# First norm summed over a host-transposed x, a column table from the host, and natural x loaded late

## The chip, the core and the metric

The kernel runs on one core of one Trainium2 chip. The core has five engines that work side by side and meet by semaphores: TensorE (PE) multiplies matrices, VectorE (DVE) and ScalarE (ACT) work element by element, GpSimd (POOL) does small odd jobs, and SyncE (SP) issues most of the loads. 16 DMA engines move data from memory to the core's SBUF; PE writes its sums to PSUM, in eight banks. The metric is the device time of one run in microseconds (us), lower being better.

## The reference

One decoder layer on 256 tokens with 1024 channels, all in float32. What matters here is its beginning:

```python
def rmsnorm(x, g):
    y = x * rsqrt(mean(x * x, axis=-1) + EPS)
    return y * g
xn = rmsnorm(h, mix_norm_g)
proj = xn @ w_in        # split into aq ak av mq mk mv mo mi mf ga gm
...                     # attention on aq ak av, an mLSTM on mq mk mv mo mi mf
h = h + merged @ w_out  # merged: both mixers, gated by ga and gm
h = h + hierarchical_moe(rmsnorm(h, ffn_norm_g))   # 32 experts, top 2 per token
```

After the experts come a small gated embedding and a last norm. The experts' weights are by far the most of what is read: some 200 of 242 MB.

## The kernel before, in words

The kernel is one straight program, whose order within each engine a scheduler fixes ahead of time: what stands earlier in the text has the higher priority among what its model thinks ready, and each engine then works through its list in order. Large tiles share a ring of ten slots (`slot`, `NRING`); a load into a ring slot waits until all that reads the slot's earlier tile is done. Loads are queued on SP in the order of the text.

*Products in two halves.* Products are made with a rounded format. So each operand is split: ACT writes the rounded upper half (`whi`, `x_hi`), DVE the rest (`wlo`, `x_lo`), and three products (hi·hi, hi·lo, lo·hi) give the sum. One split of a weight tile of 128x512 feeds twelve products of 256 columns, or six of 512. The staging tiles are three of each (`whi`, `wlo`), with two more (`spare`) from aq on.

*The start (lines 65 to 110).* x comes in its natural layout, tokens on partitions, in two halves into `h`, interleaved with the four pieces of mq's weights. Gains and biases come as rows in six small loads (`rows`), the first gain in a seventh (`g1r`), the gate biases in two more (`ifb`). Three warm products (lines 229 to 231) use `identb`, which ACT casts from `ident`.

*mq (lines 234 to 311).* PE turns `g1r` into columns, and transposes x in four groups of four products (`transpose_x`, line 253) into the "tp" banks of PSUM. For each of eight k, ACT and DVE split the transposed x (times the gain) and the weights, and PE makes twelve products into `pmq`, four tiles in PSUM: three "po" banks and one "at" bank. x is not scaled by the norm's factor; that is done when a product is copied out. The helpers `on_act` and `on_dve` chain these steps on their engines. `square_x` (line 275) lets ACT square the natural x into the scratch tile `y` and sum along the row, at k = 2 and 5. `norm_x` (line 280), at k = 6, makes the factor `r1` per token (scaling on DVE, power on POOL), and PE and DVE spread it as rows, `rT`. `load_columns` (line 244) then turns the other gains and biases into columns.

*Behind mq.* Line 548 copies `pmq` out, times `rT`. `if_gates` (line 385) makes the input and forget gates: POOL spreads their weights into the scratch `y`, 24 products go into `pif` (a "po" bank), and a chain of small steps of four partitions on DVE and ACT follows, with two scans and an exponential and a logarithm. `if_columns` (line 412) transposes the result on PE. Then come mk, aq, `conv` 0 to 2, ak, `conv` 3 to 5, av, and attention with the other projections between its heads, the mLSTM, the gates, `w_up`, `w_out` (which reads `h`) and the router. `pif`, mk and all later projections go through `proj_T` (line 323) or `proj_N`, so their splits have line 220 (ACT) and 221 (DVE).

*The experts.* For each of 32 experts 6 MB are loaded into ring slots (`load_expert`, lines 713 and 718), and PE works on them as they come.

## Time and profile before

| | before |
|---|---|
| median of 3 runs | 702.91 us (702.17 to 702.95) |
| the profiled run | 702.59 us |
| its span, first to last instruction | 701.0 us |
| PE, DVE, ACT busy, share of the span | 80%, 40%, 27% |
| moved by DMA | 242.01 MB, mean 345 GB/s |
| the chain that ended last, by engine | DMA 55%, PE 37%, DVE 4% |

All times below are of the profiled run and count from the start of its span. A busy PE is not a PE at its peak, since products are pipelined and their ends are modelled. A share of busy time is a mean over stages with different limits; each stage is read by itself.

### The profile page before, as it was taken

What the parts mean: (1) busy time and instruction counts of PE and PEld (TensorE: products, weight loads), DVE (VectorE), ACT (ScalarE), POOL (GpSimd) and SP (SyncE); (2) the same over time, 40 slices, a digit from 0 to 9 for tenths busy, and PEclk for the clock granted to TensorE, in tenths of its full rate; (3) what the DMA queues carried; (4) which work ended last, traced back from release to release, by engine and by line L of the source; (5) the groups of instructions that cost most, each with busy time, mean ns of one, the idle gap of its engine ahead of it and who ended that gap; (6) DMA issues with size and microseconds to landing.
All of it is one profiled execution on the core that took longest, in us unless ns stands there. A gap on an engine that the chain in (4) does not pass through costs nothing.

```text
span 701.0 us, 12218 instructions
## 1 busy us (share of the span) xinstructions
PE 561.0 (80%) x5161; PEld 381.0 (54%) x5161; DVE 280.6 (40%) x684; ACT 185.9 (27%) x423; POOL 38.2 (5%) x59
## 2 busy tenths in 40 slices
PE   7999999999999998595477574877666975855894
PEld 6899778899986554252233231644323442422384
DVE  4898667676665333041122014323201310401175
ACT  6575556455453211000000000010001110000263
POOL 2000000001300000000000000000000000000063
PEclk9999999999999999799789857799958998988998
DMA  7956533338777899999999999999999999999911
GB/s 252 429 226 246 223 131 121 121 121 326 309 334 301 320 429 424 427 428 425 428 426 425 428 428 424 423 426 426 426 428 421 428 427 426 427 426 426 412 70 61
DMA packets 22134, 242.01 MB, mean 345 GB/s; under 512 B 4708, under 2 KB 5304, under 8 KB 7096
## 3 DMA queue, kind: packets, MB, share of 16 engines
q1 hardware_dynamic: 22056, 241.16, 83.1%
q8 instruction: 42, 0.69, 0.4%
q14 instruction: 20, 0.16, 0.1%
q10 hardware_dynamic: 16, 0.00, 0.0%
HBM read 240.10 MB, written 1.05 MB: 344 GB/s over the span
## 4 chain that ended last, share of the span: by engine, by line
DMA 55%; PE 37%; DVE 4%; ACT 2%; issue 1%; POOL 1%; POOLq 0%; SPq 0%; DVEq 0%; ACTq 0%
DMA wt<-in_expert_gu 32%; DMA wt<-in_expert_down 17%; DMA wpp<-in_w_ple_proj 5%; PE po L331 4%; PE po L332 4%; PE po L333 4%; PE pg L811 3%; PE po L348 2%; PE po L347 2%; PE po L349 2%; PE pd L828 2%; PE px L762 1%; PE ps L840 1%; DMA wt<-in_w_mix 1%; PE pyy L471 1%
## 5 line engine op out<-in xcount | busy, mean ns | idle before, releaser
L811 PE MATMUL pg<-wt,xe 128*32 128x256 f32 x2032 | 157.8, 448 | 70.1 <-DMA wt<-in_expert_gu 70.1
L811 PEld LDWEIGHTS pg<-wt,xe 128*32 128x32 f32 x2032 | 74.5, 125 | 138.8 <-issue 58.6
L828 PE MATMUL pd<-wt,hT 128*32 128x256 f32 x1024 | 72.2, 428 | 17.2 <-DMA wt<-in_expert_down 13.1
L834 DVE COPY eo<-pd 32x256 f32<-32x256 f32 x64 | 27.1, 423 | 107.7 <-ACT eo L836 107.6
L836 ACT ACTIVATE eo<-pd 32x256 f32<-32x256 f32 x64 | 24.0, 374 | 142.2 <-PE pd L828 123.7
L828 PEld LDWEIGHTS pd<-wt,hT 128*32 128x32 f32 x1024 | 38.2, 120 | 40.7 <-issue 24.9
L817 DVE TENSOR_TENSOR hid<-sg,pg 128x128 f32<-128x128 f32 x32 | 9.2, 288 | 125.2 <-ACT sg L815 125.2
L221 DVE TENSOR_TENSOR wlo<-wt,whi 128x512 fp32r<-128x512 f32 x76 | 51.6, 686 | 18.0 <-ACT whi L220 17.7
L220 ACT ACTIVATE whi<-wt 128x512 fp32r<-128x512 f32 x77 | 47.2, 627 | 31.4 <-PE po L349 14.3
L815 ACT ACTIVATE sg<-pg 128x128 f32<-128x128 f32 x32 | 8.9, 278 | 173.1 <-PE pg L811 173.1
L762 PE MATMUL px<-og,y 128*128 128x128 f32 x256 | 37.4, 298 | 11.4 <-DVE og L753 8.0
L762 PEld LDWEIGHTS px<-og,y 128*128 128x128 f32 x256 | 33.7, 207 | 23.5 <-issue 12.7
L840 PE MATMUL ps<-eo,dwT 128*128 128x512 f32 x64 | 34.3, 662 | 8.9 <-DVE eo L834 8.8
L333 PE MATMUL po<-XT,wlo 128*128 128x256 f32 x144 | 40.2, 279 | 1.0 <-DVE wlo L221 1.0
L331 PE MATMUL po<-XT,whi 128*128 128x256 f32 x144 | 40.6, 282 | 0.0
L332 PE MATMUL po<-XT,whi 128*128 128x256 f32 x144 | 40.2, 279 | 0.0
L766 DVE TENSOR_TENSOR xe<-px,cols 128x256 f32<-128x256 f32 x32 | 13.6, 425 | 65.5 <-PE pg L811 44.2
L221 POOL TENSOR_TENSOR glo<-wt,ghi 128x1024 fp32r<-128x1024 f32 x4 | 10.6, 2664 | 446.5 <-ACT ghi L220 446.5
L333 PEld LDWEIGHTS po<-XT,wlo 128*128 128x128 f32 x144 | 27.1, 188 | 1.3 <-DVE wlo L221 1.2
L331 PEld LDWEIGHTS po<-XT,whi 128*128 128x128 f32 x144 | 27.1, 188 | 0.2 <-ACT whi L220 0.2
L221 DVE TENSOR_TENSOR spare<-wt,spare 128x512 fp32r<-128x512 f32 x34 | 23.3, 688 | 9.7 <-ACT spare L220 9.7
L332 PEld LDWEIGHTS po<-XT,whi 128*128 128x128 f32 x144 | 27.1, 188 | 0.2 <-issue 0.2
(371 smaller groups left out, 956.2 us busy)
## 6 DMA issues: line engine op xcount, KB each, us to landing
...
wt<-in_w_mix SPq DMA_DIRECT2D x10, 2048.0 KB, 22.2
...
```

What stands on the lines that cost most here:

```text
L220: a = nc.scalar.activation(dst_hi, src, AF.Copy)
L221: b = (lo_on or nc.vector).tensor_tensor(dst_lo, src, dst_hi.bitcast(F32), op=OP.subtract)
L331: mm(out[:, f], whi[:, kk], ahi[:, k], start=(k == 0), stop=False)
L332: mm(out[:, f], whi[:, kk], alo[:, k], start=False, stop=False)
L333: mm(out[:, f], wlo[:, kk], ahi[:, k], start=False, stop=(k == kn - 1))
L347: mm(outs[b], ahi[:, k, bs], whi[:, k - k0], start=(k == 0), stop=False)
L762: ins = mm(px[:, k], y[:, b, kc:kc + P], og[:, b], start=(b == 0), stop=(b == NB - 1))
L811: ins = pe(mm(pg[32 * j:32 * j + 32], xe[:, k, 32 * i:32 * i + 32], gu[k][:, :, j * P:(j + 1) * P], start=(k == 0), stop=(k == KD - 1)))
L828: pe(mm(pd[32 * c:32 * c + 32], hT[:, 32 * j:32 * j + 32], dn[j][:, c * 256:(c + 1) * 256], start=(j == 0), stop=(j == 3)))
L834: nc.vector.tensor_copy(out=dst, in_=pd[32 * c:32 * c + 32])
L836: nc.scalar.activation(dst, pd[32 * c:32 * c + 32], AF.Copy)
L840: mm(ps, dwT[0:n, b], eo[0:n, c * 512:(c + 1) * 512], start=True, stop=True)
```

## The change

x also comes transposed from the host (`xT`, channels on partitions), in three pieces, between five pieces of mq's weights, into the first half of the ring tile `QK`, which later holds attention's q and k. So PE no longer transposes x for mq. All gains and biases come as one table of columns (`cols`, 128 x 85) on ACT's queue, and the seven loads of rows, the two of the gate biases, and the transposes that made columns go. The cast of `identb` moves from ACT to DVE, and four more warm products are made.

The first norm's sum: ACT squares the transposed x in four pieces (before k = 5, 6 and 7, and after 7) into `VV`, DVE adds them up to 128 x 256, and two products with a column of ones sum over the partitions (`pss`). This stands behind mq's products, and the spreading to `rT` is a step of its own (`norm_row`) behind `pif`'s products. mq is copied out there, too. `pif` takes an "at" bank instead of a "po" bank. mk now stands ahead of `if_columns`.

Natural x is loaded in one piece into `h` behind the loads of mk, aq, ak, av, mv and mo.

```diff
--- before.py
+++ after.py
@@ -32,7 +32,7 @@
 ESTR = 256
 NITEM = 16
 NEG = -1.0e30
-NWARM0 = 3
+NWARM0 = 7
 NWARM = 27
 WARM = (7, 4, 3, 1, 3)
 LO_POOL = (11, 101)
@@ -65,42 +65,25 @@
     h = keep.tile([P, NB, D], F32, name="h")
     y = keep.tile([P, NB, D], F32, name="scratch", tag="y")
     x_v = A["x"].rearrange("o (b p) d -> p (o b) d", p=P)
-    g1r = fc.tile([KD, P], F32, name="g1r")
-    nc.scalar.dma_start(out=g1r, in_=A["mix_norm_g"].rearrange("o (k p) -> (o k) p", p=P))
-
-
+    NC_ = 85
+    cols = const.tile([P, NC_], F32, name="cols")
+    nc.scalar.dma_start(out=cols, in_=A["cols"])
+    col_of = dict(g1=0, g2=8, g3=16, cb=24, cw=32, gml=64, bg=68)
+    ifb = cols[0:36, 84:85]
+
+
+    QK = slot([P, 2, 8, T], F32, name="QK")
+    aqk, qkc = QK[:, 0], QK[:, 1]
     wts = {"mq": slot([P, KD, 512])}
     mq_v = A["w_mix"][MIX.index("mq")]
-    for i in range(4):
-        if i < 2:
-            nc.sync.dma_start(out=h[:, :, i * 512:(i + 1) * 512], in_=x_v[:, :, i * 512:(i + 1) * 512])
-        nc.sync.dma_start(out=wts["mq"][:, 2 * i:2 * i + 2], in_=mq_v[:, 2 * i:2 * i + 2])
-
-
-    rows = fc.tile([76, P], F32, name="rows")
-    col_of = {}
-    r0 = 0
-    for nm, src in (
-            ("g2", A["ffn_norm_g"].rearrange("o (k p) -> (o k) p", p=P)),
-            ("g3", A["ple_norm_g"].rearrange("o (k p) -> (o k) p", p=P)),
-            ("cb", A["conv_b"].rearrange("o (k p) -> (o k) p", p=P)),
-            ("cw", A["conv_w"].rearrange("o c (k p) -> (o c k) p", p=P)),
-            ("gml", A["mlstm_norm_g"].rearrange("o (k p) -> (o k) p", p=P)),
-            ("bg", A["b_gate"].rearrange("o (k p) -> (o k) p", p=P)),
-    ):
-        n = src.shape[0]
-        nc.sync.dma_start(out=rows[r0:r0 + n], in_=src)
-        col_of[nm] = r0
-        r0 += n
+    for (k, n), (kw, nw) in (((0, 1), (0, 1)), ((1, 3), (1, 1)), ((4, 4), (2, 2)), ((8, 0), (4, 2)), ((8, 0), (6, 2))):
+        if n:
+            nc.sync.dma_start(out=aqk[:, k:k + n], in_=A["xT"][:, k:k + n])
+        nc.sync.dma_start(out=wts["mq"][:, kw:kw + nw], in_=mq_v[:, kw:kw + nw])
 
     wif = fc.tile([P, KD, 8], F32, name="wif")
-    ifb = fc.tile([36, 1], F32, name="ifb")
-
     def load_if():
         nc.sync.dma_start(out=wif, in_=A["w_if"])
-        ifb_v = A["mlstm_if_b"].rearrange("o n -> n o")
-        nc.sync.dma_start(out=ifb[0:4], in_=ifb_v[0:4])
-        nc.sync.dma_start(out=ifb[32:36], in_=ifb_v[4:8])
 
 
     def load_cols(v):
@@ -114,7 +97,7 @@
     nc.gpsimd.affine_select(out=ident, in_=ident, pattern=[[-1, P]], compare_op=OP.not_equal,
                             fill=1.0, base=0, channel_multiplier=1)
     identb = const.tile([P, P], BF16, name="identb")
-    first_act = nc.scalar.activation(identb, ident, AF.Copy)
+    nc.vector.tensor_copy(out=identb, in_=ident)
     mhalf = const.tile([P, 8], F32, name="mhalf")
     nc.gpsimd.memset(mhalf, -0.5)
 
@@ -125,9 +108,6 @@
     RW = slot([P, 4096], F32, name="RW")
     raw = RW[:, 0:8 * (T + 3)].rearrange("p (f t) -> p f t", f=8)
     nc.gpsimd.memset(raw[:, :, 0:3], 0.0)
-    QK = slot([P, 2, 8, T], F32, name="QK")
-    nc.gpsimd.memset(QK[:, 0, 0, 0:1], 0.0)
-    aqk, qkc = QK[:, 0], QK[:, 1]
     VV = slot([P, 4096], F32, name="VV")
     av = VV[:, 0:1024].rearrange("p (b n) -> p b n", b=NB)
     smo = VV[:, 1024:2048].rearrange("p (b n) -> p b n", b=NB)
@@ -137,6 +117,7 @@
     load_if()
     for nm in ("mk", "aq", "ak", "av", "mv", "mo"):
         wts[nm] = load_cols(A["w_mix"][MIX.index(nm)])
+    nc.sync.dma_start(out=h, in_=x_v)
     YS = slot([P, 2, 2, 4, T], F32R, name="YS")
     nc.gpsimd.memset(YS[:, 0, 0, 0, 0:2].bitcast(F32), 0.0)
     ya_hi, ya_lo, ym_hi, ym_lo = YS[:, 0, 0], YS[:, 0, 1], YS[:, 1, 0], YS[:, 1, 1]
@@ -230,72 +211,55 @@
     for _ in range(NWARM0):
         warm0 = mm(pw, identb, identb[:, None, :].to_broadcast([P, 4, P]), start=True, stop=True)
 
-
-    pg1 = psf.tile([P, 512], F32, name="pg1", tag="tp")
-    after(nc.tensor.transpose(pg1[:, 0:KD], g1r, ident[0:KD, 0:KD]), warm0)
-    g1c = fc.tile([P, KD], F32, name="g1c")
-    g1_copy = nc.vector.tensor_copy(out=g1c, in_=pg1[:, 0:KD])
-    cols = const.tile([P, 76], F32, name="cols")
     bgh = fc.tile([P, 16], F32, name="bgh")
 
     def col(nm, i):
         return cols[:, col_of[nm] + i:col_of[nm] + i + 1]
 
-    def load_columns():
-        pcol = psf.tile([P, 512], F32, name="pcol", tag="tp")
-        nc.tensor.transpose(pcol[:, 0:76], rows, ident[0:76, 0:76])
-        nc.vector.tensor_copy(out=cols, in_=pcol[:, 0:76])
-        nc.vector.tensor_scalar(bgh, cols[:, col_of["bg"]:col_of["bg"] + 16], 0.5, None, op0=OP.mult)
-
 
     pmq = [psf.tile([P, T], F32, name="pmq", tag="po" if f < 3 else "at", bufs=3) for f in range(4)]
 
-    def transpose_x(k):
-        pt = psf.tile([P, 2, T], F32, name="pt", tag="tp")
-        for kk in range(2):
-            for b in range(NB):
-                after(nc.tensor.transpose(pt[:, kk, b * P:(b + 1) * P], h[:, b, (k + kk) * P:(k + kk + 1) * P], ident),
-                      warm0)
-        return pt
-
-    ss = small.tile([P, 2, NB], F32, name="ss", bufs=1)
     r1 = small.tile([P, 8], F32, name="r1", bufs=1)
     rT = fc.tile([P, T], F32, name="rT")
 
-    seq = {"act": first_act, "dve": g1_copy}
+
+    seq = {"act": nc.scalar.activation(r1, mhalf, AF.Square), "dve": None}
 
     def on_act(ins):
         after(ins, seq["act"])
         seq["act"] = ins
 
     def on_dve(ins):
-        after(ins, seq["dve"])
+        if seq["dve"] is not None:
+            after(ins, seq["dve"])
         seq["dve"] = ins
 
+    sq_x = VV[:, 0:2048].rearrange("p (i n) -> p i n", i=4)
+
     def square_x(i):
-        for b in range(NB):
-            cs = slice(i * 512, (i + 1) * 512)
-            on_act(nc.scalar.activation(y[:, b, cs], h[:, b, cs], AF.Square, accum_out=ss[:, i, b:b + 1]))
+        on_act(nc.scalar.activation(sq_x[:, i], aqk[:, 2 * i:2 * i + 2], AF.Square))
 
     def norm_x():
-        nc.vector.tensor_tensor(ss[:, 0], ss[:, 0], ss[:, 1], op=OP.add)
-        rstd_of(r1[:, 0:NB], ss[:, 0], D, NB)
-        prt = psf.tile([P, 512], F32, name="prt", tag="at", bufs=3)
+
+        for a, b in ((0, 1), (2, 3), (0, 2)):
+            on_dve(nc.vector.tensor_tensor(sq_x[:, a], sq_x[:, a], sq_x[:, b], op=OP.add))
+        on_dve(nc.vector.tensor_tensor(sq_x[:, 0, 0:T], sq_x[:, 0, 0:T], sq_x[:, 0, T:], op=OP.add))
+        pss = psf.tile([P, 512], F32, name="pss", tag="tp")
+        for b in range(NB):
+            mm(pss[:, b:b + 1], sq_x[:, 0, b * P:(b + 1) * P], ones_e[:, 0:1], start=True, stop=True)
+        rstd_of(r1[:, 0:NB], pss[:, 0:NB], D, NB)
+
+    def norm_row():
+        prt = psf.tile([P, 512], F32, name="prt", tag="tp")
         for b in range(NB):
             nc.tensor.transpose(prt[:, b * P:(b + 1) * P], r1[:, b:b + 1].to_broadcast([P, P]), ident)
         nc.vector.tensor_copy(out=rT, in_=prt[:, 0:T])
         nc.vector.tensor_scalar(r1[:, 2:4], r1[:, 0:NB], 0.5, None, op0=OP.mult)
 
-    pts = {}
     for k in range(KD):
-        if k in (0, 2, 3):
-            for kt in {0: (0, 2), 2: (4,), 3: (6,)}[k]:
-                pts[kt] = transpose_x(kt)
-        if k in (2, 5):
-            square_x(k // 4)
-        if k == 6:
-            norm_x()
-        xt, g = pts[k // 2 * 2][:, k % 2], g1c[:, k:k + 1]
+        if k in (5, 6, 7):
+            square_x(k - 5)
+        xt, g = aqk[:, k], col("g1", k)
         on_act(nc.scalar.activation(x_hi[:, k], xt, AF.Copy, scale=g))
         on_dve(nc.vector.scalar_tensor_tensor(x_lo[:, k], xt, g, x_hi[:, k].bitcast(F32),
                                               op0=OP.mult, op1=OP.subtract))
@@ -308,7 +272,9 @@
             mm(pmq[f], whi[:, f], x_hi[:, k], start=(k == 0), stop=False)
             mm(pmq[f], whi[:, f], x_lo[:, k], start=False, stop=False)
             mm(pmq[f], wlo[:, f], x_hi[:, k], start=False, stop=(k == KD - 1))
-    load_columns()
+    square_x(3)
+    norm_x()
+    nc.vector.tensor_scalar(bgh, cols[:, col_of["bg"]:col_of["bg"] + 16], 0.5, None, op0=OP.mult)
 
     spare = dict(tile=None, n=0)
 
@@ -387,8 +353,11 @@
         nc.gpsimd.memset(wif32, 0.0)
         nc.gpsimd.tensor_copy(out=wif32[:, :, 0:4], in_=wif[:, :, 0:4])
         nc.gpsimd.tensor_copy(out=wif32[:, :, 32:36], in_=wif[:, :, 4:8])
-        pif = psf.tile([P, 2, T], F32, name="pif", tag="po", bufs=3)
+        pif = psf.tile([P, 2, T], F32, name="pif", tag="at", bufs=3)
         proj_T(lambda k, f: wif32[:, k:k + 4], KD, 1, x_hi, x_lo, pif)
+        norm_row()
+        for f in range(4):
+            nc.vector.tensor_tensor(raw[:, f, 3:], pmq[f], rT, op=OP.mult)
         gpv = y.rearrange("p b (i t) -> p (b i) t", t=T)
         ipre, fpre, t0, t1, Mx = (gpv[0:4, i] for i in range(5))
         am = gpv[0:36, 5]
@@ -544,11 +513,9 @@
         return evac
 
 
-    for f in range(4):
-        nc.vector.tensor_tensor(raw[:, f, 3:], pmq[f], rT, op=OP.mult)
     if_gates()
+    chunk_T(wts["mk"], evac_raw(4))
     last_exp = if_columns()
-    chunk_T(wts["mk"], evac_raw(4))
     spare["tile"] = keep.tile([P, 2, 2, 512], F32R, name="spare", tag="y")
     chunk_T(wts["aq"], evac_q)
     for i in range(3):
@@ -1053,9 +1020,8 @@
     moe.close()
 
 
-_INS = ["x", "p", "mix_norm_g", "w_mix", "w_if", "b_gate", "conv_w", "conv_b", "mlstm_if_b", "mlstm_norm_g",
-        "w_up", "w_out", "ffn_norm_g", "router_group_w", "router_group_b", "router_expert_w", "router_expert_b",
-        "expert_gu", "expert_down", "ple_norm_g", "w_ple_gate", "w_ple_proj", "final_norm_g"]
+_INS = ["x", "xT", "p", "cols", "w_mix", "w_if", "w_up", "w_out", "router_group_w", "router_group_b",
+        "router_expert_w", "router_expert_b", "expert_gu", "expert_down", "w_ple_gate", "w_ple_proj", "final_norm_g"]
 
 
 def _laid_out(inputs):
@@ -1066,6 +1032,13 @@
     def cols(w, n):
         return w.reshape(-1, P, w.shape[1] // n, n).transpose(2, 1, 0, 3)
 
+    a["xT"] = a["x"][0].T.reshape(KD, P, T).transpose(1, 0, 2)
+    vecs = [a.pop(nm).reshape(-1, P) for nm in ("mix_norm_g", "ffn_norm_g", "ple_norm_g", "conv_b", "conv_w",
+                                                "mlstm_norm_g", "b_gate")]
+    a["cols"] = _np.zeros((P, 85), _np.float32)
+    a["cols"][:, 0:84] = _np.concatenate(vecs).T
+    ifb = a.pop("mlstm_if_b").reshape(2, HM)
+    a["cols"][0:HM, 84], a["cols"][32:32 + HM, 84] = ifb[0], ifb[1]
     w_in = a.pop("w_in")[0]
     a["w_mix"] = _np.concatenate([cols(w_in[:, IN_OFF[nm]:IN_OFF[nm] + (1024 if nm in ("ga", "gm") else 512)], 512)
                                   for nm in ("aq", "ak", "av", "mq", "mk", "mv", "mo", "ga", "gm")])
```

## Rows read from the trace of the kernel before

**Rows 1.** The page's 40 slices of 17.5 us over the whole span: what the DMA engines moved

```profile
GB/s 252 429 226 246 223 131 121 121 121 326 309 334 301 320 429 424 427 428 425 428 426 425 428 428 424 423 426 426 426 428 421 428 427 426 427 426 426 412 70 61
```

**Rows 2.** The chain of waits in order of time: start us, us, what

```profile
12.87 0.44 PE pt L257 x4
...
73.22 0.63 PE pa L444 x4
...
264.59 31.66 DMA wt<-in_expert_gu
...
656.64 1.93 PE pg L811 x32
```

**Rows 3.** The DMA queue's waits in 150 to 262 us: total us, times, longest

```profile
SPq L713 <- DVE wlo L221: 20.2, 3, 12.1
...
SPq L713 <- DMA wt<-in_expert_down: 1.1, 1, 1.1
```

**Rows 4.** Windows: stretch, us, busy and count by engine, granted clock, DMA share, GB/s

```profile
core 0: us, PE busy (x) PEld busy (x) DVE busy (x) ACT busy (x) POOL busy (x), PEclk, DMA share, GB/s
7.80:12.20 4.40, 4.39 (x20) 4.40 (x21) 3.58 (x7) 3.85 (x10) 0.00 (x0) 1.00 0.86 340
40.00:60.00 20.00, 20.00 (x177) 20.00 (x176) 20.00 (x43) 14.23 (x30) 0.10 (x1) 1.00 0.30 105
```

**Rows 5.** DMA rate in 0 to 20 us, 40 slices of 0.5 us

```profile
GB/s 0 0 0 11 99 291 221 295 303 360 254 197 303 418 410 451 426 393 426 426 426 396 246 39 53 0 0 295 164 131 197 328 426 393 459 393 426 459 459 393
```

**Rows 6.** Timeline of the start: start us, us, engine line op, names, shapes, count

```profile
1.54 1.28 ACT L117 ACT_TABLE_LOAD   x1 [1.54 <-PEq L1088]
...
3.20 1.46 PE L231 MATMUL pw<-identb 128*128 128x512 bf16 x3 [3.20 <-ACT identb L117]
...
7.81 0.55 PE L308 MATMUL pmq<-XT,whi 128*128 128x256 f32 x1 [0.62 <-ACT whi L305]
...
22.07 0.23 PE L246 MATMUL pcol<-ident,rows 76*128 76x76 f32 x1
```

**Rows 7.** Timeline, ACT's casts of weights and of x, and a square

```profile
7.04 0.63 ACT L305 ACTIVATE whi<-wt 128x512 fp32r<-128x512 f32 x1
7.57 0.46 ACT L299 ACTIVATE XT<-pt,g1c 128x256 fp32r<-128x256 f32 x1
...
8.45 0.62 ACT L278 ACTIVATE scratch<-h 128x512 f32<-128x512 f32 x1
```

**Rows 8.** Timeline of the first norm and mq's evacuation; first the scaling's line alone

```profile
L190 DVE TENSOR_SCALAR r<-ss x2: 156/488/819, 15.8 to 679.5; 128x2 f32<-128x2 f32 x2
...
16.70 1.07 POOL L191 TENSOR_TENSOR r<-r,mhalf 128x2 f32<-128x2 f32 x1
...
20.03 0.42 DVE L286 COPY rT<-prt 128x256 f32<-128x256 f32 x1
...
21.24 1.11 DVE L548 TENSOR_TENSOR RW<-pmq,rT 128x256 f32<-128x256 f32 x3 [0.20 <-PE pmq L310]
```

**Rows 9.** Timeline of PE: mk's first product and the two stalls behind it

```profile
24.92 0.28 PE L331 MATMUL po<-XT,whi 128*128 128x256 f32 x1
...
32.03 0.38 PE L333 MATMUL po<-XT,wlo 128*128 128x256 f32 x1 [1.00 <-DVE wlo L221]
...
36.16 0.28 PE L416 MATMUL pam<-ident,scratch 36*128 36x36 f32 x2 [1.46 <-DVE scratch L410]
```

**Rows 10.** Timeline: three splits on DVE, and the first use of the last two

```profile
24.50 0.68 DVE L221 TENSOR_TENSOR wlo<-wt,whi 128x512 fp32r<-128x512 f32 x1
...
39.59 0.69 DVE L221 TENSOR_TENSOR spare<-wt,spare 128x512 fp32r<-128x512 f32 x1
...
42.31 0.28 PE L333 MATMUL po<-XT,wlo 128*128 128x256 f32 x1
...
61.61 0.69 DVE L221 TENSOR_TENSOR wlo<-wt,whi 128x512 fp32r<-128x512 f32 x1
...
64.34 0.39 PE L348 MATMUL po<-wlo,XT 128*128 128x512 f32 x1
```

2 lines of the change are left out of this document (1 added, 1 removed).

## Prediction

> **What bounds the kernel now.** I read the 40 slices first. From about 245 us until near 650 us the rate sits at 412 to 429 GB/s: the experts' weights stream in, and nothing on an engine shortens that [rows 1]. The chain of waits in order of time says the same: from 264.59 us it is one DMA of expert weights after the other, until TensorE (PE) takes over at 656.64 us for the tail [rows 2]. So the end is the moment at which the stream gets going, plus fixed bytes, plus a tail that the change doesn't touch. What sets that moment? Between 157 and 245 us the rate is only 301 to 334 GB/s, so the stream is not yet full [rows 1], and the waits of the DMA queue in 150 to 262 us are for engines that still hold ring slots, the splits of old weights on VectorE (DVE) above all; DMA is among them with one wait of 1.1 us [rows 3]. A front that is X earlier frees those slots X earlier, and the end comes X earlier. I look for X.
>
> In the front PE works without a gap from 7.81 us [rows 6], apart from two stalls near 32 and 36 us [rows 9]. From 40 to 60 us PE is busy 20.00 of 20.00 us with 177 instructions, 0.113 us each, and DVE is busy 20.00 of 20.00 us too [rows 4]. That second number is the trap: whatever PE gains, DVE must follow.
>
> **The change part by part.**
>
> *Start of the mq products.* The first product starts at 7.81 us, behind the cast of the first weights, which starts at 7.04 us as they have landed [rows 6, 7]. Adding up the rate by half microseconds, the 1.05 MB up to these weights had moved at 6.1 us [rows 5], so landing is some 1.0 us behind the bytes. After the change the first product needs 0.13 MB of xT, 0.04 MB of cols and 0.26 MB of mq: 0.44 MB, moved at 3.9 us, landed at 4.9, cast by 5.5 (0.63), first product at 5.7: 2.1 us earlier. The eight transposes in front of it go. The seven warm products (three take 1.46 us, so 3.4) no longer wait for ScalarE's (ACT's) table of 1.28 us and run from about 1.9 to 5.3 us [rows 6], ahead of the data. Bounds: 5.1 us, if a smaller piece lands only 0.4 us behind its bytes, and 7.8 us, if small pieces land no sooner than the big one.
>
> Here the Trainium skill, "DMA: Bandwidth & Descriptors", section "Bandwidth", speaks against the change: batch transfers to 1 MiB or more, small ones are ruled by their descriptors. Its section "Anatomy of one DMA" gives 2.0 us fixed plus bytes over 436 GB/s, by which (an estimate) 0.44 MB from 1.41 us on land at 4.4 us, and the sum would be 0.5 us better. The trace shows 6.1 us and 1.0 more for 1.05 MB, slower than that formula.
>
> *The mq stretch.* Before, 20 PE instructions run in 7.80 to 12.20 us, 0.22 us each, which for 256 columns is the 1.2 GHz level, although the granted clock in that row reads 1.00; later ones take 0.113, the 2.4 GHz level [rows 4]. After, k=0 and k=1 run at the slow level from 5.7 to at most 10.8 us. k=2 needs 2.14 MB, moved at 8.8 us [rows 5], landed at 9.8, cast by 10.5. So from k=2 on the finer pieces help no more, DMA is the limit there, and the clock may rise anywhere before that at little loss. Six steps of 12 x 0.113 = 1.36 us follow: the end is at 18.8 (19.6 if the clock rises no sooner than at 12.2 us, as before). ACT needs 0.88 us per step from start to start and 0.62 per square [rows 7], 9.5 in all, and has 13.9. Before, the end is 22.07 us [rows 6]. Of the 3.3 us, 2.1 are the start, 0.9 two groups of four transposes inside the stretch at 0.44 [rows 2], the rest the transposes of rT that move out and the clock.
>
> *The norm.* Before, it runs beside the products, and rT is copied from 20.03 to 20.45 us [rows 8]. After, it stands behind k=7. The last square ends at 9.8 + 0.6 + 5 x 0.88 + 4 x 0.62 = 17.3 us. Two of the adds need only the squares, so from 17.1 us on three adds of 128x512 at 0.69 (a split has the same shape [rows 10]) and one of half the size at 0.42 end at 19.6. Then: two one-column products 0.3 (no row; by the transposes, 0.44 for four, 0.1 to 0.44; I take the middle), the scaling 0.16 (0.82 before, its other run 0.16), the power on GpSimd (POOL) 1.07, two transposes 0.4, the copy 0.42: rT at 22.2 [rows 8]. Four evacuations of 0.37 to 0.42 follow [rows 8]. mk's first product needs a "po" bank, and mq holds all three until the first evacuation, at 22.6.
>
> *The gate projection (pif)* no longer needs such a bank ("at" now), so it fills the wait: 24 products, 2.7 us. Its lower half is split on DVE; queued behind the adds it is ready at 20.3, so pif ends at 23.0. PE is what waits for that. mk then starts at 23.1 instead of 24.92 us [rows 9]: 1.8 us earlier, 1.2 to 3.2 by where DVE's order puts that split.
>
> *mk and after.* PE stalls at 32.03 us (1.00, for a wlo on DVE) and at 36.16 us (1.46: two transposes of the gate columns wait for DVE, with mk's products queued behind them) [rows 9]. mk now comes ahead of if_columns, so the second stall should go: 3.3 us of lead. The first stays.
>
> *What DVE allows.* I followed 17 splits from 39.59 to 61.61 us to the product that first uses them: the first ends at 40.28 and is used at 42.31, the last ends at 62.30 and is used at 64.34 [rows 10]; the leads lie between 2.0 and 3.1 us. PE can eat 2.0 us of that; more must come from DVE being earlier itself. By the terms above DVE ends mk's second split at 19.6 + 4 x 0.69 + 0.42 + 4 x 0.42 = 24.5 us; before at 25.18 [rows 10], with one conv step of 0.48 more done: 0.2 earlier at equal work, 0.7 if conv can wait. So PE's 3.3 is cut to 2.2 to 2.7, and I take 2.6, as the waits inside the gate chain leave DVE some room.
>
> *At nothing.* The late load of x (1 MB, 2.5 us at 428 GB/s) stands on SP's queue behind mo, whose load waits for mq's slot; behind it are only loads that wait longer. DMA is 0.30 busy in 40 to 60 us [rows 4], which covers it, and x is first read by the sums of w_out, behind both mixers. Without that cover it would cost at most its 2.5 us. The small DMAs of gains and biases, two transposes with their PSUM copies and POOL's wait for the squares go, all off the path.
>
> **Sum.** 702.59 us (profiled; its span is 701.0) - 2.6 = 700.0; the median of the runs, 702.91, is 0.3 above the profiled run, so 700.2.
>
> **The rivals.**
> 1. *PE keeps all of it* (-3.5 to -4.7; 698.2 to 699.4). For it: conv's steps share DVE and are not urgent, so DVE may deliver the splits first. Against it: the 20.00 of 20.00, and conv's place in the program ahead of ak and av.
> 2. *DVE takes it back* (-1.4 to +1; 701.5 to 703.9). The adds are 2.5 us more work for DVE. If it reaches mk's splits 2 us later than I have it, that alone pays for the 2.0 us of lead. The same comes out where the change does not do what it says, with pieces that land no sooner: the start stays at 7.8 us and 2.1 us of the forecast are missing.
> 3. *Slower* (+1.4 to +4; 704 to 707). The norm chain becomes the bound: mk cannot start before rT + 0.4, so from an rT later than 24.5 us on each microsecond costs one, at PE and at DVE alike. That needs the adds behind mk's first splits on DVE (three times 0.69) and the two new products ahead of pif on PE: rT near 27. Against it: the adds precede those splits in the program.
>
> **How the numbers follow.** Forecast 0.50, rival 1 0.20, rival 2 0.18, rival 3 0.12. The range, 698.3 to 703.0, takes in the forecast, nearly all of rival 1 and most of rival 2. 0.2% is 1.4 us, about what a measurement of this kernel can tell from no change: faster 0.70, same 0.18, slower 0.12.
>
> **What would show it.** First mq product at 5.7 us; mq's end at 18.8; rT at 22.2; mk's first product at 23.1; no PE stall at the gate columns; the splits' lead in 40 to 60 us down to near nothing; attention's first product at 70.6 instead of 73.22 us; PE after the stream at 654.0 instead of 656.64 [rows 2]. Wrong would be a start at 7.8, a later rT, or a front that is X earlier with an end that is not.

## The result, and the profile after

| | before | after |
|---|---|---|
| median | 702.57 us (702.17 to 702.95, 4 runs) | 709.22 us (708.11 to 709.85, 4 runs) |
| the profiled run, its span | 702.59 us, 701.0 us | 709.85 us, 708.3 us |
| mk's first product | 24.92 us | 27.58 us |
| aq, from its first product to ak's first | 10.99 us | 13.84 us |
| first load of expert weights issued | 160.40 us | 166.76 us |
| from that load to the end of the span | 540.6 us | 541.5 us |

The change makes the kernel slower: the ratio is 1.0093, with an interval of 1.0080 to 1.0106, or 6.65 us. The forecast was 2.7 us faster. The table's last rows say where the time goes: 6.4 of 7.3 us of span are lost before the first expert weights are asked for, 0.9 behind.

The slices of 17.5 us over the span and the end of the chain of waits of the changed kernel answer to [rows 1] and [rows 2]. The stream runs at the same 422 to 428 GB/s and ends in the same way; it only comes later.

```profile
GB/s 321 427 208 149 217 155 159 136 127 227 323 416 230 292 428 425 427 428 427 426 425 425 427 426 426 424 424 425 425 428 422 427 425 428 426 426 425 414 75 60
...
625.23 38.60 DMA wt<-in_expert_gu
663.87 1.93 PE pg L778 x32
```

The waits of the DMA queue in 150 to 270 us are the same too; the first of them answers to [rows 3]:

```profile
SPq L680 <- DVE wlo L202: 20.1, 3, 12.1
```

The start, from the timeline of the changed kernel (start us, us, engine line op, names, shapes, count, and what ended the idle time before), answers to [rows 6] and [rows 7]:

```profile
3.68 1.26 DVE L277 TENSOR_SCALAR bgh<-cols 128x16 f32<-128x16 f32 x1 [2.63 <-DMA cols<-in_cols]
3.76 1.24 DVE L100 CAST identb<-ident 128x128 bf16<-128x128 f32 x1
3.95 0.95 POOL L353 MEMSET scratch<- 128x1024 f32 x1
5.06 3.17 PE L212 MATMUL pw<-identb 128*128 128x512 bf16 x7 [5.06 <-DVE sel L349]
5.41 0.63 ACT L269 ACTIVATE whi<-wt 128x512 fp32r<-128x512 f32 x1 [1.17 <-DMA wt<-in_w_mix]
...
7.66 0.78 PE L272 MATMUL pmq<-XT,whi 128*128 128x256 f32 x1
...
8.84 0.63 ACT L269 ACTIVATE whi<-wt 128x512 fp32r<-128x512 f32 x1 [1.92 <-DMA wt<-in_w_mix]
...
11.67 0.63 ACT L269 ACTIVATE whi<-wt 128x512 fp32r<-128x512 f32 x1 [1.80 <-DMA wt<-in_w_mix]
```

The first weights are cast at 5.41 to 6.04 us, half a microsecond behind the forecast (landed at 4.9, cast by 5.5). The warm products run from 5.06 us on, because the identity's cast waited on DVE, and PE gets to mq at 7.66 only. The weights of k=1 and k=2 are cast when they land, at 8.84 and 11.67 us.

The norm, from the same timeline (last square, additions with two splits of pif's weights between them, sum over partitions, power, spreading, copy, mk), answers to [rows 8] and [rows 9]:

```profile
18.37 0.62 ACT L240 ACTIVATE VV<-QK 128x512 f32<-128x512 f32 x1
...
19.11 1.28 DVE L245 TENSOR_TENSOR VV<-VV 128x512 f32<-128x512 f32 x2
20.31 0.68 DVE L202 TENSOR_TENSOR wlo<-scratch,whi 128x512 fp32r<-128x512 f32 x1
20.91 0.68 DVE L245 TENSOR_TENSOR VV<-VV 128x512 f32<-128x512 f32 x1
21.52 0.68 DVE L202 TENSOR_TENSOR wlo<-scratch,whi 128x512 fp32r<-128x512 f32 x1
22.12 0.41 DVE L246 TENSOR_TENSOR VV<-VV 128x256 f32<-128x256 f32 x1
...
22.68 0.58 PE L249 MATMUL pss<-ones_e,VV 128*128 128x1 f32 x4 [0.82 <-DVE VV L246]
...
23.54 1.12 POOL L172 TENSOR_TENSOR r<-r,mhalf 128x2 f32<-128x2 f32 x1 [2.18 <-DVE r L171]
...
25.66 0.38 PE L255 MATMUL prt<-ident,r 128*128 128x128 f32 x2
...
26.08 0.42 DVE L256 COPY rT<-prt 128x256 f32<-128x256 f32 x1 [0.38 <-PE prt L255]
...
27.58 0.36 PE L297 MATMUL po<-XT,whi 128*128 128x256 f32 x1 [1.54 <-DVE RW L360]
```

Two things are to be seen. The power ends at 24.66 us, but the transposes that spread it run at 25.66 us, without any wait of PE: they stand behind pif's products in PE's list. And mk's first product waits 1.54 us for the copies of mq, which wait for `rT`.

The third place is aq. Its first stretch in the changed kernel: the timeline, then windows (stretch, us, busy and count by engine, granted clock, DMA share, GB/s).

```profile
40.67 0.31 PE L385 MATMUL pam<-ident,scratch 36*128 36x36 f32 x2
...
41.25 1.14 ACT L201 ACTIVATE spare<-wt 128x512 fp32r<-128x512 f32 x2
41.92 0.39 PE L297 MATMUL po<-XT,spare 128*128 128x256 f32 x1 [0.93 <-ACT spare L201]
41.94 1.28 POOL L202 TENSOR_TENSOR spare<-wt,spare 128x512 fp32r<-128x512 f32 x1 [17.28 <-ACT spare L201]
...
43.27 0.58 PE L299 MATMUL po<-XT,spare 128*128 128x256 f32 x1 [0.45 <-POOL YS L122]
...
40.00:45.00 5.00, 3.60 (x20) 2.95 (x19) 5.00 (x11) 3.61 (x7) 1.32 (x2) 0.81 0.85 338
45.00:50.00 5.00, 5.00 (x39) 5.00 (x39) 2.76 (x6) 3.16 (x6) 0.00 (x0) 0.85 0.04 15
```

`pam` itself no longer waits, as forecast. But `spare` is allocated in the place of the scratch tile (the tag "y"), and the scratch is what `pam` reads. So the first split into `spare` cannot be written before `pam` is through. In the kernel before, `pam` stood ahead of mk, at 36.16 us [rows 9], and mk's last products covered the split: its upper half was ready 1.8 us ahead of the first product that reads it, its lower half, made by POOL, 0.4 ahead:

```profile
36.91 0.64 ACT L220 ACTIVATE spare<-wt 128x512 fp32r<-128x512 f32 x1 [1.50 <-DVE amc L418]
37.63 1.32 POOL L221 TENSOR_TENSOR spare<-wt,spare 128x512 fp32r<-128x512 f32 x1 [16.22 <-ACT spare L220]
...
39.33 0.28 PE L331 MATMUL po<-XT,spare 128*128 128x256 f32 x1
```

In the changed kernel PE waits 0.93 us for the upper half and 0.45 us for the lower one. (The profile puts the second wait down to a small step of POOL that comes right behind this split.) Then the granted clock falls to 0.81 and 0.85: from 43.65 to about 46.2 us the products start 0.21 us apart, the 1.2 GHz level. Two waits of 1.4 us together and about as much by the clock are the 2.85 us that aq takes longer.

### The profile page after: what moved, and what is told of

Its sections match the earlier page's. It is cut to its first block, busy times and chain, and to the rows that moved or that the text cites. A ratio compares the mean times of both kernels' runs of the same rounds, so it can differ in the third digit from the quotient of the medians.

```text
span 708.3 us, 12184 instructions
## 1 busy us (share of the span) xinstructions
PE 560.8 (79%) x5151; PEld 380.8 (54%) x5151; DVE 285.4 (40%) x686; ACT 187.2 (26%) x419; POOL 37.9 (5%) x58
## 3 DMA queue, kind: packets, MB, share of 16 engines
HBM read 241.15 MB, written 1.05 MB: 342 GB/s over the span
## 5 line engine op out<-in xcount | busy, mean ns | idle before, releaser
L778 PE MATMUL pg<-wt,xe 128*32 128x256 f32 x2032 | 148.9, 428 | 70.4 <-DMA wt<-in_expert_gu 70.4
L778 PEld LDWEIGHTS pg<-wt,xe 128*32 128x32 f32 x2032 | 71.7, 120 | 133.0 <-DMA wt<-in_expert_gu 56.3
L795 PE MATMUL pd<-wt,hT 128*32 128x256 f32 x1024 | 77.4, 453 | 21.2 <-DMA wt<-in_expert_down 17.1
L202 DVE TENSOR_TENSOR wlo<-wt,whi 128x512 fp32r<-128x512 f32 x76 | 53.5, 710 | 21.3 <-ACT whi L201 20.7
```

The costliest lines, as they stand in the source:

```text
L202: b = (lo_on or nc.vector).tensor_tensor(dst_lo, src, dst_hi.bitcast(F32), op=OP.subtract)
L778: ins = pe(mm(pg[32 * j:32 * j + 32], xe[:, k, 32 * i:32 * i + 32], gu[k][:, :, j * P:(j + 1) * P], start=(k == 0), stop=(k == KD - 1)))
L795: pe(mm(pd[32 * c:32 * c + 32], hT[:, 32 * j:32 * j + 32], dn[j][:, c * 256:(c + 1) * 256], start=(j == 0), stop=(j == 3)))
```

## The experiments

All of them in one table. "aq" is the time from its first product to ak's; "load" the issue of the first expert weights; "rest" from there to the end of the span. These come from one profile of each. The kernels ran in seven series, each with the kernel before beside them; its median was between 702.01 and 702.64 us, and a ratio is taken within its series. So where medians of different series are compared, some 0.6 us can be the series, and the ratios count.

```
kernel              median  ratio   interval          mk     aq     load    rest
before              702.57                            24.92  10.99  160.40  540.6
after               709.22  1.0093  1.0080 to 1.0106  27.58  13.84  166.76  541.5
x1_order            706.65  1.0066  1.0049 to 1.0083  27.49  11.47  165.15  541.5
x2_sums             707.51  1.0080  1.0059 to 1.0100  25.23  13.88  164.65  541.3
x3_scratch          708.41  1.0086  1.0069 to 1.0103  29.20  11.32  166.30  541.3
x4_sums_order       704.15  1.0032  1.0020 to 1.0045  24.93  11.20  161.26  540.9
x5_before_mk_first  704.25  1.0025  1.0014 to 1.0037  24.20  13.85  162.92  540.7
x6_ring             704.51  1.0035  1.0020 to 1.0049  25.47  11.20  161.80  541.5
x7_start            704.03  1.0027  1.0016 to 1.0039  25.96  11.20  162.31  541.3
x8_pieces           703.41  1.0016  1.0006 to 1.0026  23.76  11.20  160.03  541.3
x9_inputs           702.20  0.9998  0.9989 to 1.0007  23.64  11.00  159.35  540.6
x10_best            703.25  1.0010  1.0001 to 1.0019  23.64  11.20  159.88  542.7
x11_best_inputs     704.51  1.0030  1.0019 to 1.0041  24.56  11.20  160.85  541.3
x12_align           700.04  0.9964  0.9951 to 0.9977  23.94  11.40  160.60  538.2
x13_before_off      706.35  1.0053  1.0039 to 1.0067  25.17  11.32  162.14  543.2
x14_after_align     705.41  1.0042  1.0029 to 1.0055  27.33  14.00  166.78  537.6
x15_before_128      700.62  0.9978  0.9969 to 0.9987  23.30  11.32  161.12  537.9
x17_after_64        707.95  1.0080  1.0066 to 1.0094  27.62  12.49  165.52  540.8
x18_best_128        699.34  0.9957  0.9944 to 0.9971  23.73  11.03  159.12  537.6
x19_before_96       705.95  1.0040  1.0026 to 1.0054  24.89  11.40  162.22  542.1
```

### The two losses in the front

x1 puts the two lines of the gate columns and mk back in their old order in the changed kernel:

```diff
-    chunk_T(wts["mk"], evac_raw(4))
     last_exp = if_columns()
+    chunk_T(wts["mk"], evac_raw(4))
```

> The changed kernel with if_columns put back ahead of mk. Theory A (the order: with mk first, the transposes of the gate columns fall to 40.67 us, and the staging tile spare, which lies in the scratch y that they read, comes free only then, so aq loses 2.8 us): the loss in aq goes, aq takes about 11.0 us from its first product to ak's instead of 13.8; the stall at the gate columns, 1.4 us, comes back in mk; total about 707 to 708, from 709.2. Theory B (only the norm chain and its extra DVE work count): aq's loss stays, the stall is added, about 710.5.

It gains 2.6 us by the medians, 1.9 by the ratios, and aq takes 11.47 us. The granted clock still drops, to 0.67 in 40 to 45 us, behind mk's stalls.

x2 squares earlier (two pieces ahead of k=2, then at 4 and 5), adds at k=3 and 6, and moves `norm_row` and the copies of mq ahead of the gates, so that the transposes no longer stand behind pif:

```diff
...
+        if k == 2:
+            square_x(0)
+            square_x(1)
+        if k == 3:
+            on_dve(nc.vector.tensor_tensor(sq_x[:, 0], sq_x[:, 0], sq_x[:, 1], op=OP.add))
+        if k in (4, 5):
+            square_x(k - 2)
+        if k == 6:
+            norm_x()
...
-    square_x(3)
-    norm_x()
+    norm_row()
+    for f in range(4):
+        nc.vector.tensor_tensor(raw[:, f, 3:], pmq[f], rT, op=OP.mult)
...
```

> The changed kernel with the squares ahead of k=2, 4 and 5, the adds at k=3 and 6 and the spreading to rT and mq's copying out ahead of the gate projection; the same number of instructions. Theory B (the norm stands behind k=7 and holds mq's three PSUM banks and with them mk): rT ends near 20.5 instead of 26.5 us, mk's first product comes at about 24.3 instead of 27.58, total about 706.0. Rival (the adds are too much work for DVE wherever they stand): mk starts near 26, total within 1 us of 709.2.

mk comes at 25.23 us, 2.35 earlier, between the two expectations. aq is as slow as in the changed kernel (13.88), so the order of the gate columns is a loss of its own. The total gains 1.7 us by the medians and 0.9 by the ratios, whose intervals overlap.

x3 leaves the order as changed, but puts the gates' small rows into a free part of `VV` instead of the scratch tile, so that `spare` waits for nothing:

```diff
-        gpv = y.rearrange("p b (i t) -> p (b i) t", t=T)
+        gpv = VV[:, 0:2048].rearrange("p (i t) -> p i t", t=T)
...
-        am = y.rearrange("p b (i t) -> p (b i) t", t=T)[0:36, 5]
+        am = VV[:, 0:2048].rearrange("p (i t) -> p i t", t=T)[0:36, 5]
```

> The changed kernel with the gates' small rows in the tile VV instead of the scratch y, so that spare (which takes y's place) no longer waits for the gate columns; the order is the changed one. Theory A: aq's first split into spare no longer waits for 40.67 us, aq takes about 11.2 us instead of 13.8, total about 706.5. Rival (aq's loss comes from late splits on DVE and ACT, not from the tile): aq still takes 13 us or more, total within 1 us of 709.2.

aq takes 11.32 us: the shared place is the cause of its waits. The total hardly moves, for a reason that neither theory had. The splits for `spare` are now ready so early that the scheduler puts one ahead of the norm on DVE, beside one on POOL. Its timeline:

```profile
25.98 1.26 POOL L202 TENSOR_TENSOR spare<-wt,spare 128x512 fp32r<-128x512 f32 x1 [1.33 <-ACT spare L201]
26.39 1.39 DVE L202 TENSOR_TENSOR spare<-wt,spare 128x512 fp32r<-128x512 f32 x1 [0.71 <-ACT spare L201]
27.71 0.41 DVE L256 COPY rT<-prt 128x256 f32<-128x256 f32 x1
```

A split of 0.69 takes 1.39 us beside POOL's, `rT` is ready at 28.12 instead of 26.50 us, and mk starts at 29.20; the granted clock then falls to 0.67 in 30 to 35 us. The loss was moved, not removed. This agrees with the Trainium skill, "SBUF — State Buffer", section "SBUF: two separate sides": DVE with two inputs from SBUF and POOL reading it take one port pair by turns, and the loser waits for the whole instruction.

x4 takes x1 and x2 together:

> Early sums and the old order together. If A and B are two separate losses they add up: mk's first product at 24.3 us, aq in 11 us, total 702.5 to 704. If both are one loss seen twice (DVE as the bound): no better than the better one of the two alone.

The front is back where it was (mk 24.93, aq 11.20), and 5.07 of the 6.65 us with it (4.3 of 6.5 by the ratios): the two causes are separate, and without both most of the loss is gone. Together they bring more than x1 and x2 added up (4.3 by the medians, 2.8 by the ratios). x1 and x2 each still have a stretch of 5 us at a granted clock of 0.67 and 0.66, in 40 to 45 us; in x4 it is 1.00 from 25 to 50 us.

x5 asks for the order from the other side. It makes mk come ahead of the gate columns in the kernel before, which is the one edit that the prediction valued at 1.46 us of gain:

```diff
-    last_exp = if_columns()
     chunk_T(wts["mk"], evac_raw(4))
+    last_exp = if_columns()
```

> The kernel before with one edit, the one the prediction valued at a gain of 1.46: mk goes ahead of the gate columns. Theory A (the spare staging tile shares its place with the scratch y, so with the columns behind mk its first split waits for the column transposes, and aq pays for it even where the norm is early): the stall of 1.46 at 36.16 is gone and aq starts near 37.9, but aq then takes some 13.8 in place of 11.0, as it did in the changed kernel; the sum is +1.4, 703.4. Rival (aq's loss comes from the norm's lateness only): aq takes 11.0 and the kernel gains the 1.46, 700.6. It also tells whether a product pitch of 0.1175 in place of 0.1133 belongs to the chip or to the changed kernel.

```profile
35.03 0.39 PE L333 MATMUL po<-XT,wlo 128*128 128x256 f32 x1 [0.63 <-DVE wlo L221]
...
37.74 0.31 PE L416 MATMUL pam<-ident,scratch 36*128 36x36 f32 x2
...
38.93 0.39 PE L331 MATMUL po<-XT,spare 128*128 128x256 f32 x1 [0.88 <-ACT spare L220]
...
40.28 0.38 PE L333 MATMUL po<-XT,spare 128*128 128x256 f32 x1 [0.84 <-POOL YS L141]
...
41.00:46.00 5.00, 5.00 (x32) 5.00 (x31) 3.21 (x7) 2.92 (x8) 0.00 (x0) 0.66 0.64 259
```

The kernel gets 1.8 us slower with the norm as early as ever. The timeline and the window show the same two waits, and behind them a granted clock of 0.66. They also show a wait of 0.63 us for a split on DVE, at 35.03 us, that the kernel before does not have: with the stall at the gate columns gone, PE got to that product ahead of DVE.

### The start

x6 gives out the ring's tiles in the old order (mq's weights, XT, RW, QK), on top of x4:

> x4 with the ring's tiles given out in the order of the kernel before (weights of mq, XT, RW, QK, VV); nothing else is moved. Theory A (what is left of the loss, some 1.2 to 2.1, comes from where QK, XT and the mq weights lie, by the waits of later loads or by the pace of the products): att0 back from 72.8 to 72.5, the expert loads from 161.3 to 160.4, 702.3. Rival (the place does nothing): as x4, 704.1.

Nothing that stands out: 704.51 beside 704.15 us, ratios 1.0035 and 1.0032.

x7, on top of x4, casts the identity on ACT again and keeps the halved gate bias out of DVE's start:

```diff
-    nc.vector.tensor_copy(out=identb, in_=ident)
+    first_act = nc.scalar.activation(identb, ident, AF.Copy)
...
-    nc.vector.tensor_scalar(bgh, cols[:, col_of["bg"]:col_of["bg"] + 16], 0.5, None, op0=OP.mult)
+    on_dve(nc.vector.tensor_scalar(bgh, cols[:, col_of["bg"]:col_of["bg"] + 16], 0.5, None, op0=OP.mult))
```

> x4 with the identity cast for the warm products on ScalarE, as in the kernel before, and the gate bias halved on VectorE behind the norm's additions instead of at the very start. Theory A (the transfers set mq: the weights of k=2 are copied at 11.7 whatever the start): warm products from about 3.2, first mq product 6.2 in place of 7.67, the granted clock up about 1.4 earlier, mq's end earlier by at most 0.3, 703.9. Rival (the start sets it): mq's end earlier by 1.4 and everything behind with it, 702.7.

x8, also on top of x4, loads the transposed x in two pieces and mq in four, of 0.5 MB each:

```diff
-    for (k, n), (kw, nw) in (((0, 1), (0, 1)), ((1, 3), (1, 1)), ((4, 4), (2, 2)), ((8, 0), (4, 2)), ((8, 0), (6, 2))):
+    for (k, n), (kw, nw) in (((0, 4), (0, 2)), ((4, 4), (2, 2)), ((8, 0), (4, 2)), ((8, 0), (6, 2))):
```

> x4 with the transposed x loaded in two pieces and the weights of mq in four, as the kernel before had them (0.5 MB each). Theory A (the small first pieces lower the rate of the first 10 us to 240 to 350 GB/s): weights of k=2 copied near 10.0 in place of 11.7, k=0 hardly later, mq's end earlier by about 1.3, 702.8. Rival (the rate is the same and only the order differs): k=0 about 0.8 later, k=2 near 11, mq's end within 0.3 of x4's, 704.1.

The casts of mq's weights on ACT, first x7 (k = 0, 1, 2), then x8 (k = 1, 2):

```profile
4.70 0.63 ACT L276 ACTIVATE whi<-wt 128x512 fp32r<-128x512 f32 x1 [0.45 <-DMA wt<-in_w_mix]
...
9.16 0.63 ACT L276 ACTIVATE whi<-wt 128x512 fp32r<-128x512 f32 x1 [2.63 <-DMA wt<-in_w_mix]
...
12.25 0.63 ACT L276 ACTIVATE whi<-wt 128x512 fp32r<-128x512 f32 x1 [1.02 <-DMA wt<-in_w_mix]
```

```profile
7.22 0.61 ACT L276 ACTIVATE whi<-wt 128x512 fp32r<-128x512 f32 x1
...
10.03 0.63 ACT L276 ACTIVATE whi<-wt 128x512 fp32r<-128x512 f32 x1 [0.76 <-DMA wt<-in_w_mix]
```

x7 starts mq at 5.61 us, the 5.7 of the prediction, and gains nothing that stands out (704.03, ratios 1.0027 and 1.0032): mq ends at 23.07 us, no sooner than in x4 (22.04), with k=2 cast at 12.25 (x4: 11.20). (mq's end is read where pif's first product starts.) x8 starts at 8.16 us, later than x4's 7.67, and ends mq at 20.87, 1.2 earlier, with k=2 cast at 10.03. Its median is 0.74 us lower than x4's, 1.1 by the ratios, whose intervals overlap.

The profiles of the other kernels settle what the totals leave open. In all nine kernels with x2's sums mq ends 10.80 to 10.86 us behind the cast of k=2, whenever mq started. That cast comes at 11.20 to 12.25 us in the nine kernels with the small pieces, and at 9.91 to 10.87 in the five with x8's. So the transfers set the end of mq, and the small pieces made them late.

### The rest

x8 seemed to have its front ahead of the kernel before, as its loads of experts were asked for 0.4 us earlier, and still it took 0.9 us longer by the medians. (x9 shows below that two profiles of the same instructions can differ by more than 0.4.) Three reasons were tried. x9 gives the kernel before the input tensors of the changed one (xT and the column table declared and not read):

> The kernel before, instruction for instruction, but with the input tensors of the changed kernel in its order (xT and the column table are declared and not read; the eight small inputs that the change drops stand last). Theory A (the weights lie elsewhere in the chip's memory, and the experts' stream runs some 0.15% slower for it: x8 gets its first expert loads 0.3 to 0.4 earlier than the kernel before and its last ones 0.3 later): front as before, expert loads from 160.4, last ones later by 0.6, 703.2. Rival (the inputs do nothing, and the 0.7 comes from the changed kernel's own instructions): 702.5.

x10 is x8 with x7's start and eleven warm products:

> x8 (sums early, columns ahead of mk, pieces of 0.5 MB) with the identity cast on ScalarE and eleven warm products, so that the clock is up before the first mq product. Theory A (with big pieces the products of mq are no longer held by transfers behind the first, so the slow products at its start are pure loss): first product near 7.7 at 0.117 apart, mq's end 1.0 earlier than in x8, the expert loads 1.0 earlier, 702.4. Rival (as in x7, an earlier start only opens a gap in front of k=2 and the end of mq comes no sooner): 703.4.

x11 is x10 with the old input tensors in their old order, and xT and the table behind them:

> x10 with the input tensors of the kernel before in their old order, and xT and the column table behind them. Theory A (the place of the weights costs 0.7): 701.7, 0.7 below x10, with the same front to within 0.1. Rival (the inputs do nothing): as x10.

x9 differs from the kernel before by nothing that can be measured. It also says how far a single profile of the front can be trusted: with the same instructions its mk starts 1.28 us earlier than in [rows 9], and its first expert load comes 1.05 us earlier. What rests on less than that is read from medians here. x10 starts mq at 6.96 us, 1.2 earlier than x8, and ends it at 20.75, 0.1 earlier: no gain that stands out. x11 is 1.26 us slower than x10, against both expectations; its first mq product comes at 8.75 us, 1.8 later. Why, these runs do not tell.

The third reason was found in the addresses. Within each partition the tiles lie in pools, one behind the other. `cols` grew from 76 to 85 columns (304 to 340 bytes, which take 320 and 352 in steps of 32) in the pool that lies below the ring of weight tiles. By the allocation the ring starts at byte 36064 of each partition instead of 36032. x12 pads `cols` to 92 columns in x10 (and a small tile from 8 to 16), by which the ring starts at 36096. (The padded columns of a changed kernel are loaded too: 28 bytes per partition more, 108 in x17 below.) x13 pads the kernel before so that its ring is at 36064 (and the pools behind it 64 bytes on); x14 pads the changed kernel to 36096.

```diff
-    NC_ = 85
+    NC_ = 92
...
-    r1 = small.tile([P, 8], F32, name="r1", bufs=1)
+    r1 = small.tile([P, 16], F32, name="r1", bufs=1)[:, 0:8]
```

> x10 with the column table padded from 85 to 92 columns and the small norm tile r1 from 8 to 16, and nothing else: by the allocation the ring of weight tiles then starts at byte 36096 of each partition, a multiple of 64 as in the kernel before (36032), in place of 36064. Theory A (weights that land 32 bytes off a multiple of 64 are written slightly slower, and that is the 0.75 that the changed kernel and its variants lose between their first expert loads and their last): the loads' lead of the front is kept to the end, 702.5, 0.0 to 0.1% over the kernel before. Rival (the place within 64 bytes does nothing): as x10, 703.3.

> The kernel before with its column tile padded from 76 to 84 columns (and r1 from 8 to 16), so that its ring starts at byte 36064, where the changed kernel's does; no instruction is changed. Theory A (see x12): it loses 0.7 in the stream of the experts and some 0.5 between 72 and 160 us, 703.4 to 703.7. Rival: 702.5.

> The changed kernel with only the two paddings of x12. Theory A: 0.7 to 1.2 less than the changed kernel, a ratio of 1.0080 in place of 1.0093. Rival: 1.0093.

The effect is there and three to five times as large as expected: 3.2 us less for x12 and 3.8 less for x14 by 32 bytes, 4.0 more for x13. It also was not what had been expected: x12 and x14 do not return to the rate of the kernel before but pass it. So the kernel before, at 36032, is itself not at the best place. x15 puts it at 36096, x17 the changed kernel at 36160 (the same place within 128 bytes as 36032), x18 is x12 with the pools behind the ring placed as in x15, and x19 is x13 with those pools unmoved:

> The kernel before with two tiles padded (cols to 92 columns, r1 to 24) so that its ring starts at byte 36096 of each partition, a multiple of 128, where x12 and x14 have it, in place of 36032, a multiple of 64 only; everything behind the ring keeps its place within 128 bytes. No instruction is changed. Theory A (what counts is the ring's start within 128 bytes: at 0 the experts' stream runs at 430 GB/s, as in x12 and x14, and at 64 and 96 at 426): 430 GB/s, a stream 2.6 to 3.3 shorter, 699.5. Rival (only the changed kernel gains by it): 702.4.

> The changed kernel with two tiles padded so that its ring starts at byte 36160, which lies within 128 bytes where the kernel before has it (64); it is the change without its shift of the ring. Theory A (the places 64 and 96 differ by 0.7 to 3.7 us, by x13): ratio 1.005 to 1.008, 706 to 708. Rival (64 and 96 are alike, and x13's loss has another reason): as the changed kernel, 1.0093, 709.

> x12 with one more padding, so that what lies behind the ring has the place within 128 bytes that x15 gives it: the best version of the change beside the kernel before, both with the ring on a multiple of 128. Theory A (the front of the best version is 0.5 to 0.9 earlier, the stream alike): 0.5 to 0.9 below x15, near 699.0. Rival (the gain of x12 is the ring's place alone): as x15.

> The kernel before with its ring at byte 36064 of each partition, where the changed kernel has it, as in x13, but with the pools behind the ring kept at a multiple of 128 as in the kernel before (x13 had moved them to 64 as well): cols padded to 84 columns, r1 to 32. No instruction is changed. Theory A (the ring's place costs the 1.3 that x17 showed, and the other 2.4 of x13 came with the pools behind the ring): 703.8, ratio 1.002. Rival (the ring's place alone costs the kernel before what x13 showed): 706.2, ratio 1.005.

The window of 265 to 650 us, in which the experts stream in, of before (ring at 36032), x19 (36064), x15 and x14 (36096); the last number is GB/s:

```profile
265.00:650.00 385.00, 266.12 (x2860) 139.69 (x2852) 84.24 (x235) 32.64 (x91) 0.00 (x0) 0.85 1.01 426
```

```profile
265.00:650.00 385.00, 258.39 (x2866) 136.46 (x2869) 86.17 (x243) 32.58 (x91) 0.00 (x0) 0.88 1.01 426
```

```profile
265.00:650.00 385.00, 259.89 (x2889) 137.51 (x2881) 86.26 (x242) 33.33 (x93) 0.00 (x0) 0.87 1.01 429
```

```profile
265.00:650.00 385.00, 265.75 (x2875) 139.76 (x2873) 88.81 (x246) 32.64 (x91) 0.00 (x0) 0.86 1.01 430
```

The "rest" of the table sorts the twenty kernels by the ring's place: 537.6 to 538.2 us at 36096 (four kernels), 540.6 to 540.8 at 36032 and 36160 (four), 540.9 to 543.2 at 36064 (twelve). The pool that holds `h`, the scratch and `spare` lies right below the ring and moved with it each time, so the runs do not tell the two apart; that it is the ring is argued from the stream, which is written to the ring alone.

So the kernel before wins 1.9 us by place alone (x15). x18, with the repaired change and its ring at the same place, stands 1.3 us below that (698.25 to 699.82, beside 700.07 to 702.16 in the same series). It is the best version: 3.15 us below the kernel before, 0.9957. But the 1.3 us are not shown to be the change's: in the profiles x18's mk starts 0.43 us later than x15's, and its lead arises behind mk, where the two do the same work.

There the place acts in a second way, on the pace of PE. The window of 40 to 60 us, as in [rows 4], of before, x19, x15 and x18:

```profile
40.00:60.00 20.00, 20.00 (x177) 20.00 (x176) 20.00 (x43) 14.23 (x30) 0.10 (x1) 1.00 0.30 105
```

```profile
40.00:60.00 20.00, 20.00 (x171) 20.00 (x170) 20.00 (x43) 14.27 (x30) 0.10 (x1) 1.00 0.29 104
```

```profile
40.00:60.00 20.00, 20.00 (x172) 20.00 (x171) 20.00 (x44) 13.61 (x27) 0.10 (x1) 1.00 0.30 108
```

```profile
40.00:60.00 20.00, 20.00 (x176) 20.00 (x176) 19.96 (x43) 13.64 (x28) 0.10 (x1) 1.00 0.30 100
```

PE is busy all the time and the clock is granted in full, yet the first three, which differ by no instruction, get 177, 171 and 172 products done. The table's aq sorts in the same way, where no wait disturbs it: 10.99 and 11.00 us in before and x9, 11.03 in x18, 11.20 in x4, x6, x7, x8, x10 and x11 (all laid out as the changed kernel is), and 11.32 to 11.40 in x12, x13, x15 and x19. x12 has x18's instructions at about the pace of x15: its ratio is 0.9964 beside x15's 0.9978, with intervals that overlap. So no run shows that the repaired change gains anything at an equal pace.

x17 and x19 size the shift from 36032 to 36064. Put into the kernel before it costs 3.3 us (x19). Taken out of the changed kernel it gives 1.3 (x17; the intervals of the two ratios overlap), and of that most is the clock: in x17 the granted clock stays up behind aq's waits, in 40 to 50 us its PE gets 70 products done where the changed kernel gets 59.

```profile
40.00:45.00 5.00, 3.60 (x26) 2.95 (x25) 5.00 (x11) 3.77 (x8) 1.32 (x2) 1.00 0.82 324
45.00:50.00 5.00, 5.00 (x44) 5.00 (x43) 4.16 (x9) 3.61 (x7) 0.10 (x1) 1.00 0.03 9
```

Whether the clock falls there is not decided by the place alone (it fell in x14 as well), so the share of the shift in the 6.65 us stays open between 1.3 and 3.3. At equal places the change as it was made costs 5.5 us (x17 against before), 4.8 (x14 against x15, from two series) or 3.3 (after against x19, from two series). In 50 to 60 us PE gets 87 products done in x17 and 90 in the kernel before, but 87 and 87 in the second pair and 88 and 87 in the third. So the 5.5 hold a difference of pace as well, and 3.3 to 4.8 are the fairer figures.

## Why the prediction was wrong, step by step

**What bounds the kernel: right.** The front came 6.4 us later and the end 7.3 us later, with the same waits of the DMA queue for old weights' splits (20.1 us, before 20.2). One assumption in it was wrong: that bytes behind that point cost a fixed time. They cost 537.6 to 543.2 us, for the most part by where they land.

**The start: the landing right, the start of PE wrong, the worth wrong.** The first weights were cast from 5.41 us on, where the forecast had them landed at 4.9; eight other kernels with the same first pieces began the cast at 4.52 to 4.95, so the estimate of the landing was good. The warm products came at 5.06 us and not at 1.9: the edit moves the identity's cast from ACT to DVE, and the prediction counted what it no longer waits for and not what it is queued behind on DVE, where a small step that waits for `cols` comes first, and POOL clears the scratch beside it (1.24 us for the cast). x7 shows that the 2.1 us would have been worth nothing anyway.

**The mq stretch: the step that failed is "k=2 landed at 9.8".** It took the rate of the old pieces for the new ones. k=2 was cast at 11.67 instead of about 9.9, mq ended at 21.35 instead of 18.8 us. In 6 to 10 us the DMA engines moved 328 and 308 GB/s, in the kernel before 395 and 418. x8 shows that the pieces made k=2 late: with pieces of 0.5 MB the same bytes are there sooner, and it is cast at 10.03. But x8, too, moves only 332 and 350 GB/s in 6 to 10 us, so something else than the number of pieces keeps the rate there below the kernel before; no run tells what. The rule that spoke against the change, to batch transfers to 1 MiB or more (the Trainium skill, "DMA: Bandwidth & Descriptors", section "Bandwidth"), pointed the right way. Its reason, the descriptors, is given there for transfers under 64 KB; the smallest piece here has 0.13 MB, and no run shows the reason. The prediction used the trace against the rule only for the first 0.44 MB.

**The norm: the step that failed is the sum to `rT`, 22.2 us; it came at 26.50.** The last square was 1.7 us late (18.99 for 17.3), by the weights of k=2. The additions ended at 22.53 for 19.6, as two splits of pif went between them. The spreading came 1.0 us after the power had ended, because its transposes stand behind pif in PE's list. The prediction had pif end at 23.0 us and `rT` ready at 22.2, and did not see that the second contradicts the first. (Its terms also add up to 21.95 us and not to 22.2, which changes nothing.) x2 shows the three together at 2.35 us of mk's start.

**mk ahead of the gate columns: the step that failed is "the second stall should go".** It went, and a dearer one came: 1.4 us of waits and about 1.4 us of clock at aq. The prediction followed who waits for `pam`, and not who waits for the tile that `pam` reads. x5 shows it alone: +1.8 us instead of -1.46.

**What DVE allows** was not put to the test in the changed kernel, as PE never got ahead. x5 speaks for it: with the stall of 1.46 us gone, PE waits 0.63 us for a split on DVE. The size of the cap, 2 us, is neither shown nor refuted.

**At nothing: one entry was missing.** The wider column table was not on the list. Nine columns shifted every weight tile by 32 bytes. The late load of x was rightly there: it landed 26.9 us behind its issue at 19.59 us, and from 24 to 52 us no wait of PE is for a transfer.

**The rivals.** The third came in its mechanism, `rT` late and mk bound to it. Its condition came only in part: the additions fell among pif's splits, not behind mk's, and the transposes behind pif did the rest. It had been given 0.12 since "the adds precede those splits in the program". The order of the text is what the scheduler starts from, not what it ends with. It priced the time at 704 to 707; the second loss, at aq, carried it to 709. (The forecast's own last step is 0.1 off: 702.91 - 2.6 is 700.3.)
